# Three 256-column matmuls for a k tile in place of one of 512 and one of 256, with no folding of halves

## The chip, the cores and the metric

The kernel runs on one core of a Trainium2 chip. The metric is the device time of one execution in microseconds (us), the median over three timed runs. One more execution, on its own, is taken by the hardware profiler; its trace is what the views quoted here show.

## The reference, cut to what matters

One layer of an encoder block on 256 tokens of width 2048, in float32: a combined input projection, windowed attention with 12 query and 4 key/value heads of 128, a Fourier group, an output projection with a residual, and a feed-forward part with a width-3 convolution on its gate.

```python
h = _rmsnorm(x, norm1_g)
proj = h @ w_in                       # q 1536, k 512, v 512, u 512 columns
a = _rmsnorm(_window_attention(q, k, v, sink), attn_out_g)
f = _rmsnorm(_fourier_mix(u, w_fourier), fourier_out_g)
x = x + jnp.concatenate([a, f], axis=-1) @ w_out
up = _rmsnorm(x, norm2_g) @ w_up      # gate and value, 5504 columns each
gate = depthwise_conv(gate, dw_w, width 3) + dw_b
x = x + (gelu(gate) * val) @ w_down
return _rmsnorm(x, normf_g)
```

## The kernel before, in words

Every product is made of three, so that it comes out near float32: each operand is held as a high part and a low part (type fp32r, four bytes an element), and high times high, high times low and low times high are summed in PSUM. Weights arrive as tiles of 128 x 2048 float32, one megabyte each (`raw`, three buffers). `split_parts` makes the parts from such a tile: ScalarE (ACT) copies it into the high part (L170) and VectorE (DVE) subtracts that from the tile into the low part (L171). Both parts lie in one buffer (`parts_tile`, three buffers): the high part begins at one of `PLACES`' first numbers, the low part 2048 elements and the second number behind the buffer's start, in elements of four bytes.

There are two kinds of product. In the first, `moving_weights` and the products of the down-projection (`by_parts`, L1019 to L1021), the weights stream through TensorE in 512 columns and the activations are loaded as the stationary operand. In the second, `still_weights`, it is the weights that are loaded, 128 x 128 at a time, and the activations that stream: 256 tokens. The second kind makes q and k (16 units, one for a head, in the order `QK_ORDER`) and gate and value (43 units each, one for 128 of the 5504 columns), which is 102 units in all. The activations `hT` (for q and k) and `hU` (for gate and value) hold, for each of the 16 k tiles, the 256 high columns and behind them the 256 low columns.

A unit of `still_weights` before the change does two matmuls for a k tile. One loads the high part of the weights and streams all 512 columns (L326), so that high times high lies in the left half of the PSUM bank and high times low in the right half. The other loads the low part and streams the 256 high columns into the left half (L328). `lag=4`, for q, k and the first gate after the pair, lets five high matmuls go before the first low one; at the end of such a unit five low ones stand in a row. Since the sum then lies in two halves, ScalarE copies the right half to SBUF and VectorE adds the left half to it: `qk_out` (L579, L581) and `scaled_sum` (L810, L812). After that keys are multiplied by `r1b`, gate and value by `r2b` (L813).

The order of the work is written out by hand. `unit` issues the matmuls of unit i and then what stands beside it: the steps of attention heads that are at other stages, and the splitting of the weights of unit i + 2. In the feed-forward part a list of items does the same, in which gate and value units take turns with the products of the down-projection (`PATTERN`); `ff_step` runs the posts of earlier items, `scaled_sum` one item behind its matmuls, `gate_conv` two behind, and splits the weights of item n + 2. Each engine does its instructions in the order in which they were issued.

Three other places stream 256 columns with a load for each matmul: the scores (L602, six a head), the values (L674, six a head) and the Fourier rows (L491, 24 in a row); the very last product of the kernel does it too (L1156 to L1158, in two pieces of 256 columns).

Of the kernel before, what the change touches and what calls it, by code (L numbers as in the profile page):

```python
# [8 lines left out]
F32 = mybir.dt.float32  # L9
F32R = mybir.dt.float32r  # L10
AF = mybir.ActivationFunctionType
ALU = mybir.AluOpType

P = 128
D = 2048
S = 256
NK = D // P
# [46 lines left out]
def ff_items():  # L64


    def ups(tiles):
        return [(kind, j) for j in tiles for kind in ("gate", "val")]

    items = ups(range(8))  # L70
    for g in range(N_GROUPS):
        todo = {
            "u": ups(range(8 * g + 8, 8 * g + 16)),
            "s": [("product", g, c, p) for c in range(2) for p in PRODUCTS[c]],
        }
        items += [todo[c].pop(0) for c in PATTERN]
        assert not any(todo.values())
    items += [("down", 0, c) for c in range(4)] + ups(LAST)
    items += [("down", 1, c) for c in range(4)] + [("last", c) for c in range(4)]
    return items  # L80
# [3 lines left out]
def block_kernel(  # L84
# [18 lines left out]
    nc = tc.nc  # L103
# [10 lines left out]
    def bank(pool, name):  # L114
        return pool.tile([P, 512], F32, tag=pool.name, name=name)
# [5 lines left out]
    items, up_index = ff_items(), {}  # L121
# [11 lines left out]
    raws, halves = {}, {}  # L133


    PLACES = {"still": (0, 16), "first": (16, 16), "moving": (0, 0), "product": (28, 28)}

    def parts_tile(name, place):
        t = wp.tile([P, 2 * 2048 + 128], F32R, tag="parts", name=name, bufs=3)
        oh, ol = PLACES[place]  # L140
        return t[:, oh : oh + 2048], t[:, 2048 + ol : 4096 + ol]

    def load(i, pieces=1):
        if i < len(units) and i not in raws:
            src, n, _ = units[i]
            raws[i] = wp.tile([P, 2048], F32, tag="raw", name=f"raw{i}", bufs=RAW)
            m = n // pieces
            for p in range(pieces):
                s = slice(p * m, (p + 1) * m)
                nc.sync.dma_start(raws[i][:, s], src[:, s])  # L150
                yield
# [28 lines left out]
    ph = pa.enter_context(tc.tile_pool(name="pa", bufs=1))  # L180
# [21 lines left out]
    first = load(0, 4)  # L202
# [50 lines left out]
    ps = bank(dn, "ps_warm")  # L253
# [58 lines left out]
                ps, ah, wl, start=False, stop=last and q == q0 + len(kk) - 1  # L312
            )

    def still_weights(hi, lo, ps, kk, lag=0):


        todo = [("hi", k) for k in kk[: lag + 1]]
        for n, k in enumerate(kk):
            todo.append(("lo", k))  # L320
            todo += [("hi", q) for q in kk[lag + 1 + n : lag + 2 + n]]
        for part, k in todo:
            h = hT[k // 4][:, k % 4, :]
            s = slice(k * P, (k + 1) * P)
            if part == "hi":
                nc.tensor.matmul(ps, hi[:, s], h, start=k == 0, stop=False)  # L326
            else:
                nc.tensor.matmul(  # L328
                    ps[:, 0:S], lo[:, s], h[:, 0:S], start=False, stop=k == NK - 1
                )  # L330

    def hk(k):
# [15 lines left out]
    before, beside, behind = {}, {}, {}  # L348

    def at(when, i, f, *a):  # L350
        when.setdefault(i, []).append((f, a))
# [5 lines left out]
    def unit(i, work):  # L357
        run(before, i)
        work(*halves.pop(i))
        run(beside, i)  # L360
        step(i)
        run(behind, i)
# [6 lines left out]
    for k in range(NK):  # L369
        c, q = k // 4, k % 4  # L370
# [4 lines left out]
        hi, lo = halves[c]  # L375
# [49 lines left out]
    r1b = ph.tile([P, S], F32, tag="r1b", name="r1b")  # L425
# [137 lines left out]
    for c in range(4):  # L563

        def work(hi, lo):
            for b in range(2):
                moving_weights(
                    hi, lo, 512, range(4 * c, 4 * c + 4), hk, b, ps_v[b], c == 0, c == 3
                )

        unit(N_V + c, work)


    qk_sb, st = {}, {}
    sq_a = ph.tile([P, S], F32, tag="sq", name="sq_a")

    def qk_out(kind, h, ps):
        tmp = ph.tile([P, S], F32, tag="tmp", name=f"tmp_{kind}{h}", bufs=2)
        nc.scalar.activation(tmp, ps[:, S : 2 * S], AF.Copy)  # L579
        add = ph.tile([P, S], F32, tag="add", name=f"add_{kind}{h}", bufs=2)  # L580
        nc.vector.tensor_tensor(add, ps[:, 0:S], tmp, ALU.add)  # L581
        if kind == "k":
            nc.vector.tensor_tensor(add, add, r1b, ALU.mult)
        st["add", kind, h] = add

    def qk_parts(kind, h):

# [99 lines left out]
    for i in range(N_QK, N_OUT + 8):  # L687
        heads = {i - s: h for (kind, h), s in slot_of.items() if kind == "q"}
        new = [kh for kh, s in slot_of.items() if i - s == 1]
        if 5 in heads:  # L690
            at(before, i, values, heads[5])
        if 4 in heads:
            at(before, i, turn, heads[4])
        if 2 in heads:
            at(before, i, scores, heads[2])
        if 3 in heads:
            at(beside, i, weigh, heads[3])
        for kind, h in new:
            at(beside, i, lambda k=kind, h=h: qk_out(k, h, st.pop(("ps", k, h))))
        if 5 in heads:  # L700
            at(beside, i, values_out, heads[5])
        if 4 in heads:
            at(beside, i, turn_out, heads[4])
        for kind, h in new:
            at(beside, i, qk_parts, kind, h)
        if 2 in heads:
            at(beside, i, scores_out, heads[2])
            at(behind, i, exps, heads[2])

    fourier_channels_steps()  # L710
    for n, (kind, h) in enumerate(QK_ORDER):

        def work(hi, lo):
            ps = st["ps", kind, h] = bank(mm, f"ps_{kind}{h}")
            still_weights(hi, lo, ps, range(NK), lag=4)

        unit(N_QK + n, work)

# [49 lines left out]
    for n, (c, kq) in enumerate(OUT_ORDER):  # L768
        i = N_OUT + n
# [14 lines left out]
        if kq >= 2:  # L784
            part = "a" if kq == 2 else "f"
            ps = ps_a[c] if kq < 3 else ps_a[c, "f"]
# [15 lines left out]
    fp = ctx.enter_context(tc.tile_pool(name="fp", bufs=2))  # L802
    hT[:] = hT2
    r2b = fp.tile([P, S], F32, tag="r2b", name="r2b", bufs=1)
# [1 line left out]
    gate_out, sums_of, act = {}, {}, {}  # L806

    def scaled_sum(ps, name):
        tmp = fp.tile([P, S], F32, tag="ftmp", name=f"ft_{name}")
        nc.scalar.activation(tmp, ps[:, S : 2 * S], AF.Copy)  # L810
        add = fp.tile([P, S], F32, tag="fadd", name=f"fa_{name}", bufs=3)
        nc.vector.tensor_tensor(add, ps[:, 0:S], tmp, ALU.add)  # L812
        nc.vector.tensor_tensor(add, add, r2b, ALU.mult)  # L813
        sums_of[name] = add

    def gate_conv(j):
# [83 lines left out]
    def ring_load():  # L900
        if ring_next[0] < len(ring):
            key = ring[ring_next[0]]
            ring_next[0] += 1
            ring_tiles[key] = fp.tile([P, 2048], F32, tag="rawd", name="rawd%d%d%s" % key)
            nc.sync.dma_start(ring_tiles[key], weights_of(*key))
# [174 lines left out]
    for q in range(2):  # L1080
        kind, j = items[q]
        ps = bank(mm, f"ps_{kind}{j}")
# [6 lines left out]
    for ps, hi, lo in pair:  # L1089
        still_weights(hi, lo, ps, range(12, NK))  # L1090
# [7 lines left out]
    for n, it in enumerate(items):  # L1098
        if n < 2:
            continue  # L1100
        if it[0] == "last":
            break
        if n in (8, 9):
            ring_load()
        if n == 13:
            pending.append(lambda: first_sums(0, 0))
        if it[0] in ("gate", "val"):
            kind, j = it
            ps = bank(mm, f"ps_{kind}{j}")
            still_weights(*halves.pop(up_index[n]), ps, range(NK), lag=4 if n == 2 else 0)  # L1110
            ff_step(n)
            up_posts(n, kind, j, ps)
            continue
        if it[0] == "product":
            kind, g, c, p = it
            end = g == N_GROUPS - 1
            if (c, p) in held:
                by_parts(held[c, p], parts[p], *halves.pop(it), g == 0, end)
            else:
                ps = bank(mm, f"ps_{p}{g}{c}")  # L1120
                by_parts(ps, parts[p], *halves.pop(it), True, True)
                at(beside, n + 1, product_out, g, c, p, ps)
            if end and p == "N4":
                at(behind, n + 1, shared_out, c)
        else:
            kind, g, c = it
            hi, lo = halves.pop(up_index[n])
            ps = [bank(mm, f"ps_l{g}{c}{b}") for b in range(2)]
            for b in range(2):
                moving_weights(hi, lo, 512, LATE[g], act.get, b, ps[b], True, True)  # L1130
            at(beside, n + 1, down_out, c, ps)
            if (g, c) == (0, 0):
                gfb = fp.tile([P, D], F32, tag="sumw", name="gfb", bufs=1)
                nc.gpsimd.dma_start(gfb, normf_g.partition_broadcast(P))
        ff_step(n)
# [3 lines left out]
    i = up_index[n]  # L1139
# [145 lines left out]
```

## Time and profile before

| what | us |
|---|---|
| median of 3 runs | 952.24 |
| lowest and highest | 951.86, 952.95 |
| the profiled execution, its own time | 953.02 |
| its span, first to last instruction | 951.2 |
| TensorE busy in it | 940.7 |
| VectorE busy | 744.8 |
| ScalarE busy | 540.3 |

PE is TensorE's matmuls, PEld its weight loads, DVE VectorE, ACT ScalarE, POOL GpSimd. A row of groups gives line, engine, operation, output and inputs, shapes and count, then busy us and mean ns of one, then the idle time before and what ended it. A row of the timeline gives start, duration, engine, line and what was done; the time from one start to the next is what a matmul costs in a stream, since matmuls overlap and their recorded ends are modelled. The granted TensorE clock was 0.998 of full speed over the span.

### The profile page before, as it was taken

How to read it: one execution, taken by the hardware profiler on the slowest of the kernel's cores; microseconds unless marked ns; L12 is line 12 of the kernel's file. 1: busy time of each engine (PE TensorE's matmuls, PEld its weight loads, DVE VectorE, ACT ScalarE, POOL GpSimd, SP SyncE). 2: the span in 40 equal slices, each digit the busy share in tenths (PEclk: the TensorE clock that was granted, in tenths of full speed). 3: DMA queues.
4: the chain of work that ended last, by engine and by line, in shares of the span. 5: the costliest groups of instructions: out<-in, count | busy, mean ns of one | idle time of the engine just before them, and what ended most of it. 6: DMA issues, size and time to landing. Idle time of an engine off the chain costs nothing.

```text
span 951.2 us, 12801 instructions
## 1 busy us (share of the span) xinstructions
PE 940.7 (99%) x5089; PEld 813.0 (85%) x5089; DVE 744.8 (78%) x924; ACT 540.3 (57%) x654; POOL 44.7 (5%) x59
## 2 busy tenths in 40 slices
PE   8999999999999999999999999999999999999996
PEld 7788999888888888888888888888888888888885
DVE  5667878667676779887898877998889979888774
ACT  5846666544464456655555555565556755653444
POOL 0000000000000000000000000000000000000003
PEclk9999999999999999999999999999999999999999
DMA  8844444445556675978687787777987696765542
GB/s 313 346 180 178 147 164 140 171 177 177 183 177 216 265 240 202 260 254 282 214 271 232 239 291 257 251 238 223 295 253 245 213 294 201 243 241 205 197 133 89
DMA packets 33548, 211.59 MB, mean 222 GB/s; under 512 B 3792, under 2 KB 4304, under 8 KB 9424
## 3 DMA queue, kind: packets, MB, share of 16 engines
q1 hardware_dynamic: 29744, 184.54, 52.1%
q0 software_dynamic: 3600, 26.22, 14.2%
q8 instruction: 40, 0.66, 0.2%
q14 instruction: 20, 0.16, 0.1%
q10 hardware_dynamic: 144, 0.01, 0.0%
HBM read 208.65 MB, written 2.10 MB: 222 GB/s over the span
## 4 chain that ended last, share of the span: by engine, by line
PE 92%; DVE 3%; DMA 2%; issue 1%; ACT 1%; SPq 0%; POOL 0%; ACTq 0%; POOLq 0%
PE ps_val L326 16%; PE ps_gate L326 16%; PE ps_val L328 8%; PE ps_gate L328 8%; PE ps_q L326 5%; PE ps_P L1020 3%; PE ps_P L1021 3%; PE ps_P L1019 3%; PE ps_q L328 2%; PE ps_a L311 2%; PE ps_a L309 2%; PE ps_a L310 2%; PE ps_N L1021 2%; PE ps_N L1020 2%; PE ps_N L1019 2%; DMA raw<-in_w_in 2%
## 5 line engine op out<-in xcount | busy, mean ns | idle before, releaser
L171 DVE TENSOR_TENSOR parts<-raw,parts 128x2048 fp32r<-128x2048 f32 (+3 forms) x145 | 313.1, 2159 | 62.5 <-ACT parts L170 62.5
L170 ACT ACTIVATE parts<-raw 128x2048 fp32r<-128x2048 f32 (+3 forms) x144 | 262.0, 1820 | 72.4 <-PE ps_l L311 25.9
L326 PE MATMUL ps_val<-hU,parts 128*128 128x512 f32 x688 | 236.2, 389 | 0.0
L326 PE MATMUL ps_gate<-hU,parts 128*128 128x512 f32 x688 | 235.8, 389 | 0.0
L328 PE MATMUL ps_val<-hU,parts 128*128 128x256 f32 x688 | 189.9, 276 | 0.0
L328 PE MATMUL ps_gate<-hU,parts 128*128 128x256 f32 x688 | 189.3, 276 | 0.0
L326 PEld LDWEIGHTS ps_val<-hU,parts 128*128 128x128 f32 x688 | 129.2, 188 | 26.6
L326 PEld LDWEIGHTS ps_gate<-hU,parts 128*128 128x128 f32 x688 | 129.1, 188 | 26.7
L328 PEld LDWEIGHTS ps_val<-hU,parts 128*128 128x128 f32 x688 | 129.2, 188 | 1.2 <-DVE parts L171 0.2
L328 PEld LDWEIGHTS ps_gate<-hU,parts 128*128 128x128 f32 x688 | 128.9, 188 | 1.2
L810 ACT ACTIVATE ft_g<-ps_gate 128x256 f32<-128x256 f32 x43 | 16.5, 384 | 116.6 <-PE ps_gate L328 116.6
L810 ACT ACTIVATE ft_v<-ps_val 128x256 f32<-128x256 f32 x43 | 16.5, 384 | 88.3 <-PE ps_val L328 88.3
L326 PE MATMUL ps_q<-hT,parts 128*128 128x512 f32 x192 | 61.3, 393 | 0.0
L1019 PE MATMUL ps_P<-parts_P,op_P 128*128 128x512 f32 x128 | 49.8, 389 | 0.0
L1020 PE MATMUL ps_P<-parts_P,op_P 128*128 128x512 f32 x128 | 49.8, 389 | 0.0
L1021 PE MATMUL ps_P<-parts_P,op_P 128*128 128x512 f32 x128 | 49.8, 389 | 0.0
L328 PE MATMUL ps_q<-hT,parts 128*128 128x256 f32 x192 | 45.5, 278 | 0.0
L916 DVE TENSOR_TENSOR parts_N<-sumw,parts_N 128x2048 fp32r<-128x2048 f32 x16 | 36.6, 2290 | 10.1 <-ACT parts_N L915 10.1
L326 PEld LDWEIGHTS ps_q<-hT,parts 128*128 128x128 f32 x192 | 35.2, 188 | 6.8
L309 PE MATMUL ps_a<-parts,cat 128*128 128x512 f32 x96 | 37.9, 394 | 0.0
L1021 PE MATMUL ps_N<-parts_N,op_N 128*128 128x512 f32 x96 | 37.5, 390 | 0.1
L311 PE MATMUL ps_a<-parts,cat 128*128 128x512 f32 x96 | 37.5, 390 | 0.0
(323 smaller groups left out, 1564.7 us busy)
## 6 DMA issues: line engine op xcount, KB each, us to landing
raw<-in_w_up SPq DMA_DIRECT2D x86, 1024.0 KB, 5.0
raw<-in_w_in SPq DMA_DIRECT2D x21, 1024.0 KB, 4.9
raw<-in_w_out SPq DMA_DIRECT2D x16, 1024.0 KB, 4.8
sumw<-in_w_down POOLq DMA_DIRECT2D x16, 1024.0 KB, 8.4
raw<-in_w_down_late SPq DMA_DIRECT2D x8, 1024.0 KB, 4.8
raw<-in_w_down_last SPq DMA_DIRECT2D x4, 768.0 KB, 4.2
raw<-in_w_in SPq DMA_DIRECT2D x8, 256.0 KB, 6.5
xs<-in_x SPq DMA_DIRECT2D x4, 512.0 KB, 11.1
```

What stands on the lines that cost most here:

```text
L170: nc.scalar.activation(hi[:, s], raw[:, s], AF.Copy)
L171: nc.vector.tensor_tensor(lo[:, s], raw[:, s], f32(hi[:, s]), ALU.subtract)
L309: nc.tensor.matmul(ps, ah, wh, start=first and q == q0, stop=False)
L310: nc.tensor.matmul(ps, al, wh, start=False, stop=False)
L311: nc.tensor.matmul(ps, ah, wl, start=False, stop=last and q == q0 + len(kk) - 1)
L326: nc.tensor.matmul(ps, hi[:, s], h, start=k == 0, stop=False)
L328: nc.tensor.matmul(ps[:, 0:S], lo[:, s], h[:, 0:S], start=False, stop=k == NK - 1)
L810: nc.scalar.activation(tmp, ps[:, S : 2 * S], AF.Copy)
L916: nc.vector.tensor_tensor(lo, src, f32(hi), ALU.subtract)
L1019: nc.tensor.matmul(ps, o[:, 0, p, :], hi[:, s], start=first and p == 0, stop=False)
L1020: nc.tensor.matmul(ps, o[:, 1, p, :], hi[:, s], start=False, stop=False)
L1021: nc.tensor.matmul(ps, o[:, 0, p, :], lo[:, s], start=False, stop=last and p == 3)
```

## The change

For q, k, gate and value each k tile now takes three matmuls of 256 columns, all summed in the same 256 columns of PSUM: high weights by high activations, high weights by low activations, low weights by high activations. Each matmul loads its own weights. The copy of the right half and the addition go: `scaled_sum` multiplies PSUM by `r2b`, keys are multiplied by `r1b` straight from PSUM, and the parts of a query are made straight from PSUM. The low parts of these weights lie 128 bytes further than 2048 elements from the buffer's start, where they lay 64 bytes further. `lag` is gone.

```diff
-    PLACES = {"still": (0, 16), "first": (16, 16), "moving": (0, 0), "product": (28, 28)}
+    PLACES = {"still": (0, 32), "first": (16, 16), "moving": (0, 0), "product": (28, 28)}
...
-    def still_weights(hi, lo, ps, kk, lag=0):
-        todo = [("hi", k) for k in kk[: lag + 1]]
-        for n, k in enumerate(kk):
-            todo.append(("lo", k))
-            todo += [("hi", q) for q in kk[lag + 1 + n : lag + 2 + n]]
-        for part, k in todo:
+    def still_weights(hi, lo, ps, kk):
+        for k in kk:
             h = hT[k // 4][:, k % 4, :]
             s = slice(k * P, (k + 1) * P)
-            if part == "hi":
-                nc.tensor.matmul(ps, hi[:, s], h, start=k == 0, stop=False)
-            else:
+            for n, (w, o) in enumerate([(hi, 0), (hi, S), (lo, 0)]):
                 nc.tensor.matmul(
-                    ps[:, 0:S], lo[:, s], h[:, 0:S], start=False, stop=k == NK - 1
+                    ps[:, 0:S], w[:, s], h[:, o : o + S],
+                    start=k == 0 and n == 0, stop=k == NK - 1 and n == 2,
                 )
...
-    def qk_out(kind, h, ps):
-        tmp = ph.tile([P, S], F32, tag="tmp", name=f"tmp_{kind}{h}", bufs=2)
-        nc.scalar.activation(tmp, ps[:, S : 2 * S], AF.Copy)
-        add = ph.tile([P, S], F32, tag="add", name=f"add_{kind}{h}", bufs=2)
-        nc.vector.tensor_tensor(add, ps[:, 0:S], tmp, ALU.add)
+    def qk_out(kind, h):
+        ps = st.pop(("ps", kind, h))[:, 0:S]
         if kind == "k":
-            nc.vector.tensor_tensor(add, add, r1b, ALU.mult)
-        st["add", kind, h] = add
+            add = ph.tile([P, S], F32, tag="add", name=f"add_{kind}{h}", bufs=2)
+            nc.vector.tensor_tensor(add, ps, r1b, ALU.mult)
+            ps = add
+        st["add", kind, h] = ps
...
-            still_weights(hi, lo, ps, range(NK), lag=4)
+            still_weights(hi, lo, ps, range(NK))
...
     def scaled_sum(ps, name):
-        tmp = fp.tile([P, S], F32, tag="ftmp", name=f"ft_{name}")
-        nc.scalar.activation(tmp, ps[:, S : 2 * S], AF.Copy)
         add = fp.tile([P, S], F32, tag="fadd", name=f"fa_{name}", bufs=3)
-        nc.vector.tensor_tensor(add, ps[:, 0:S], tmp, ALU.add)
-        nc.vector.tensor_tensor(add, add, r2b, ALU.mult)
+        nc.vector.tensor_tensor(add, ps[:, 0:S], r2b, ALU.mult)
         sums_of[name] = add
...
-            still_weights(*halves.pop(up_index[n]), ps, range(NK), lag=4 if n == 2 else 0)
+            still_weights(*halves.pop(up_index[n]), ps, range(NK))
```

More of the change, by code (lines that the diff above doesn't have):

```diff
@@ L698, in block_kernel @@
         for kind, h in new:
-            at(beside, i, lambda k=kind, h=h: qk_out(k, h, st.pop(("ps", k, h))))
+            at(beside, i, qk_out, kind, h)
         if 5 in heads:
```

## The prediction

> **What bounds the kernel now.** I read the page first: busy times, the clock, and the shares of the chain that ended last.
>
> ```profile
> span 951.2 us, 12801 instructions
> PE 940.7 (99%) x5089; PEld 813.0 (85%) x5089; DVE 744.8 (78%) x924; ACT 540.3 (57%) x654; POOL 44.7 (5%) x59
> PEclk9999999999999999999999999999999999999999
> PE 92%; DVE 3%; DMA 2%; issue 1%; ACT 1%; SPq 0%; POOL 0%; ACTq 0%; POOLq 0%
> ```
>
> TensorE is busy for 99% of the span, its clock granted at nine tenths or more all along, and it carries 92% of the chain. But a busy share does not say that TensorE waits for nobody, so I looked next at who it waited for, in the waits of PE and PEld. Apart from the first tens of microseconds, where the first weights land, these three are the only ones that VectorE's work for the changed part can touch (columns: who waited for whom, total us, times, longest):
>
> ```profile
> PEld ps_N L1021 <- DVE parts_N L916: 0.5, 1, 0.5
> PEld ps_val L328 <- DVE parts L171: 0.2, 1, 0.2
> ...
> PE ps_l L309 <- DVE xs L1026: 0.2, 1, 0.2
> ```
>
> So VectorE's work reaches TensorE for 0.9 us in all. The kernel is bound by how fast TensorE can be fed with matmuls, and the question is what the changed stream costs from one matmul's start to the next. The timeline of PE at the start and the end of one gate unit and one product:
>
> ```profile
> 501.57 0.39 PE L326 MATMUL ps_gate<-hU,parts 128*128 128x512 f32 x1
> 501.80 0.28 PE L328 MATMUL ps_gate<-hU,parts 128*128 128x256 f32 x1
> 501.91 0.39 PE L326 MATMUL ps_gate<-hU,parts 128*128 128x512 f32 x1
> ...
> 507.01 0.39 PE L1019 MATMUL ps_N<-parts_N,op_N 128*128 128x512 f32 x1
> ...
> 509.73 0.39 PE L326 MATMUL ps_val<-hU,parts 128*128 128x512 f32 x1
> ```
>
> From 501.57 to 507.01 the unit takes 5.44 us, 0.340 for each of 16 k tiles. Twelve matmuls of 512 columns take 509.73 - 507.01 = 2.72, 0.2267 each. That leaves 0.340 - 0.2267 = 0.1133 for the one of 256: half of 0.2267, so in this alternation time goes by columns and the loads are hidden.
>
> **The change, part by part: the matmuls.** A k tile streams 512 + 256 = 768 columns before and 3 x 256 = 768 after. By columns alone nothing changes. What is added is one matmul and one weight load for a k tile. The load cannot be saved because the same high part comes twice: the scores also use the same weights twice in a row, then others, and load every time (the one line's instructions):
>
> ```profile
> L602 PEld LDWEIGHTS ps_s<-kT,qT x72: 187/189/192, 75.5 to 172.5; 128*128 128x128 f32 x72
> L602 PE MATMUL ps_s<-kT,qT x72: 278/282/368, 75.7 to 172.6; 128*128 128x256 f32 x72
> ```
>
> 72 loads for 72 matmuls. Now look at when loads happen, in the timeline of PEld for the gate unit above:
>
> ```profile
> 501.80 0.19 PEld L326 LDWEIGHTS ps_gate<-hU,parts 128*128 128x128 f32 x1
> 501.92 0.19 PEld L328 LDWEIGHTS ps_gate<-hU,parts 128*128 128x128 f32 x1
> 502.14 0.19 PEld L326 LDWEIGHTS ps_gate<-hU,parts 128*128 128x128 f32 x1
> ```
>
> A load starts when the matmul before its own starts. In the alternation the load of the low part has 0.227 of a 512-column matmul to hide in, that of the high part only 0.113. After the change every load has 0.113. So the rows to price it are those where 256-column matmuls with their own loads follow each other: the end of a query unit with `lag`, then values and scores; the Fourier rows in the chain; the last product:
>
> ```profile
> 136.56 0.76 PE L328 MATMUL ps_q<-hT,parts 128*128 128x256 f32 x5
> 137.15 0.40 PE L674 MATMUL ps_o<-pt,v_hi 128*128 128x256 f32 x2
> ...
> 137.87 0.88 PE L602 MATMUL ps_s<-kT,qT 128*128 128x256 f32 x6
> 138.59 1.31 PE L326 MATMUL ps_k<-hT,parts 128*128 128x512 f32 x5
> ...
> 49.01 2.88 PE ps_f L491 x24
> ...
> 941.27 0.28 PE L1157 MATMUL ps_e<-hi,act 128*128 128x256 f32 x1
> ...
> 942.47 0.28 PE L1158 MATMUL ps_e<-lo,act 128*128 128x256 f32 x1
> ```
>
> Six scores take 138.59 - 137.87 = 0.72, 0.120 each; six values 137.87 - 137.15 = 0.72, again 0.120; 24 Fourier rows 2.88, 0.120; ten of the last product 942.47 - 941.27 = 1.20, 0.120. Five low parts of the very weights in question take 137.15 - 136.56 = 0.59, which is 0.113 for the first (its successor's load still profits from the long matmul ahead) and 0.119 for each of the other four. Four places in different buffers agree on 0.0067 more than a column count gives. I take 0.113 for the first and 0.120 for each of the other 47 matmuls of a unit: 5.75 us in place of 5.44.
>
> The units are 102 and the k tiles 1632, from these groups (mean ns is the second number after the bar):
>
> ```profile
> L326 PE MATMUL ps_val<-hU,parts 128*128 128x512 f32 x688 | 236.2, 389 | 0.0
> L326 PE MATMUL ps_gate<-hU,parts 128*128 128x512 f32 x688 | 235.8, 389 | 0.0
> L328 PE MATMUL ps_gate<-hU,parts 128*128 128x256 f32 x688 | 189.3, 276 | 0.0
> L326 PE MATMUL ps_q<-hT,parts 128*128 128x512 f32 x192 | 61.3, 393 | 0.0
> L328 PE MATMUL ps_q<-hT,parts 128*128 128x256 f32 x192 | 45.5, 278 | 0.0
> L326 PE MATMUL ps_k<-hT,parts 128*128 128x512 f32 x64 | 20.4, 393 | 0.0
> ```
>
> 688 + 688 + 192 + 64 = 1632, and 1632 / 16 = 102. Units of q and k run a little slower than 5.44: their matmuls are 393 - 389 = 4 ns longer for 256 wide ones and 278 - 276 = 2 ns for 256 narrow ones, 1.5 us in sum; that is the row of five and five that `lag` makes, and it goes. Before: 102 x 5.44 + 1.5 = 556.4. After: 102 x 5.75 = 586.5. Difference **+30.1 us**, all of it on the path, since TensorE is the path. Bounds: 0.118 for every matmul (the mean of the five low ones) gives 48 x 0.118 x 102 = 577.7, +21; 0.1205 gives 590.0, +34.
>
> **The copies and additions.** They go from 86 gate and value units and 16 of q and k:
>
> ```profile
> L812 DVE TENSOR_TENSOR fa_g<-ps_gate,ft_g 128x256 f32<-128x256 f32 x43 | 18.1, 422 | 24.1 <-ACT ft_g L810 24.1
> L810 ACT ACTIVATE ft_g<-ps_gate 128x256 f32<-128x256 f32 x43 | 16.5, 384 | 116.6 <-PE ps_gate L328 116.6
> ```
>
> 102 x 0.42 = 43 us less on VectorE, 102 x 0.38 = 39 us less on ScalarE. Nearly all of it lies beside TensorE's work, so it is worth at most the 0.9 us of waits above; I count -0.5, because a slower TensorE lets VectorE catch up. If TensorE should stay as fast, VectorE's waits go as well. Multiplying by `r2b` straight from PSUM costs what the addition cost, which also read PSUM. The additions' buffer and the PSUM banks come free earlier; nobody waited for either.
>
> **`lag` gone.** The low part of the first k tile is wanted 0.23 us into a unit, not at the sixth matmul. Gate and value units had no lag but for one, and for the unit at 501.57 VectorE had the low part finished at 498.17 + 2.29 = 500.46:
>
> ```profile
> 498.17 2.29 DVE L171 TENSOR_TENSOR parts<-raw,parts 128x2048 fp32r<-128x2048 f32 x1
> ```
>
> That is 1.3 us before 501.80, in the stretch where VectorE is fullest. I count it at nothing; its cover is the two units between splitting and use, and without it each unit could lose up to the 0.9 us that `lag` covered, 16 us over 17 units. The 64 further bytes of the low parts cost no instruction; what they may do is a rival's matter.
>
> Sum: 30.1 - 0.5 is about +30. The profiled execution took 953.0 (1.8 more than its span), which gives 983; the median of 952.2 gives **982**. A measurement of this kernel can tell about 0.2%, 1.9 us, from no change.
>
> **Rivals.** *The loads fit* (other sign). Where the two parts of the weights lie against the streaming activations is not the same in any of my four rows as after the change, and the low part's place is moved in this very edit. If the 0.0067 is a clash between load and stream that this place avoids, then each matmul costs 0.1133, a unit 5.44, the stream 554.9: -1.5, and the waits another -0.9 at most: 952.2 - 2.4 = 949.8, near 950. It decides at 0.1138: up to there, 48 x 102 x 0.0005 = 2.4 us are covered by what is saved. For it: in the alternation a load that has just 0.113 is in time, 16 times a unit, with the high part at its unchanged place. Against it: there each is followed by one that has 0.227, and with the second tight load in a row the spacing goes to 0.119. I give it 0.38, 0.27 of that faster by over 0.2% and 0.11 within 0.2%, as the saving is close to the line.
>
> The Trainium skill has a rule that speaks for this rival: "TensorE: Matmul & The Clock Gate", section "LDWEIGHTS (loading the stationary operand)", gives a load as its columns divided by 1.2 in ns. For 128 columns that is an estimate of 107 ns, which would fit under a matmul of 113, and by it the result would be 950. The rows above with 0.120 do not agree with it as long as loads follow each other this closely.
>
> *Something between*: the clash is eased but not gone, 0.115 to 0.118 a matmul, +8 to +21: 960 to 973. Chance 0.07.
>
> *Loads in a row do not overlap*: each took 0.19 in the rows above. If a matmul cannot start before its load's recorded end and loads follow one another, a k tile costs 3 x 0.188 = 0.564, and 1632 x 0.224 = 366 us are added: 1318. The scores speak against it, 0.120 with loads of 0.189. Chance 0.01.
>
> *VectorE had been the hidden bound*, so that 43 us less of it shows: 952.2 - 5 or more. The waits of 0.9 us in all speak against it; it lies within the 0.27.
>
> **How the numbers follow.** Forecast 0.54, with its own range 973 to 986 (from +21 to +34); fitting loads 0.38; between 0.07; loads in a row 0.01. Slower by over 0.2%: 0.54 + 0.07 + 0.01 = 0.62. Leaving out the fitting loads would leave out 0.38, so the range goes from them to the forecast's upper end: 948.5 (1.5 under 950, for savings in q and k that I undercounted) to 986.
>
> **What would show it.** In the profile after, PE and PEld rows x5089 become x6721 (+1632). A gate unit on the timeline takes 5.75 from its first start to the next item's. The spacing inside it is 0.120, and PE stays at 99%; VectorE's busy time falls by some 43 us and ScalarE's by 39, their shares further. Wrong: a spacing of 0.113 and a unit of 5.44 mean that the loads fit; a PEld wait for VectorE's `parts` at L171 of several microseconds means that `lag` had been needed.

## The result and the profile after

The changed kernel takes 959.73 us, the kernel before 952.29 (medians of four runs each): a ratio of 1.0077, 95% interval 1.006 to 1.0095. That is +7.4 us, slower as forecast, but a quarter of the +30 that was forecast, and outside the 973 to 986 given for the forecast's own case. The profiled execution took 959.13 with a span of 957.4.

The page of the changed kernel, the same lines as before the change:

```profile
span 957.4 us, 15831 instructions
PE 947.8 (99%) x6721; PEld 884.8 (92%) x6721; DVE 703.0 (73%) x822; ACT 510.5 (53%) x552; POOL 44.6 (5%) x59
PE 96%; DMA 2%; ACT 0%; DVE 0%; issue 0%; POOL 0%; ACTq 0%; POOLq 0%; SPq 0%
```

TensorE does 1632 matmuls and loads more, VectorE is busy for 41.8 us less and ScalarE for 29.8 less, and TensorE still carries the chain. By the starts of their matmuls the 102 units together take 556.8 us before and 564.1 after, 7.3 more. What VectorE made TensorE wait for at L916, L171 and L1026 in the body of the kernel is gone; what is left of PEld's waits for VectorE and ScalarE lies in the first 30 us, where the first weights land. Its longest rows:

```profile
PEld ps_u L311 <- DVE parts L171: 1.7, 4, 0.5
PEld ps_u L309 <- ACT parts L170: 1.2, 2, 0.7
```

So where do the 6 us of span come from? I cut the span at the same five instructions in both traces: the first gate unit after the pair, the first unit behind the first product, the first late down-projection, the first unit of the last stretch, the first matmul of the last product. The timeline of PE, of the kernel before and then of the changed one:

```profile
272.96 0.48 PE L326 MATMUL ps_gate<-hU,parts 128*128 128x512 f32 x1
...
368.29 0.39 PE L326 MATMUL ps_val<-hU,parts 128*128 128x512 f32 x1
...
850.18 0.39 PE L309 MATMUL ps_l<-parts,act 128*128 128x512 f32 x1
...
872.43 0.39 PE L326 MATMUL ps_gate<-hU,parts 128*128 128x512 f32 x1
...
926.88 0.39 PE L1156 MATMUL ps_e<-parts,act 128*128 128x512 f32 x1
```

```profile
273.32 0.36 PE L322 MATMUL ps_gate<-hU,parts 128*128 128x256 f32 x1
...
373.19 0.28 PE L322 MATMUL ps_val<-hU,parts 128*128 128x256 f32 x1
...
854.64 0.39 PE L309 MATMUL ps_l<-parts,act 128*128 128x512 f32 x1
...
876.63 0.28 PE L322 MATMUL ps_gate<-hU,parts 128*128 128x256 f32 x1
...
932.64 0.39 PE L1147 MATMUL ps_e<-parts,act 128*128 128x512 f32 x1
```

| stretch | before, us | after, us | difference |
|---|---|---|---|
| up to gate 1 | 272.96 | 273.32 | +0.36 |
| 17 gate and value units, then the first product | 95.33 | 99.87 | +4.54 |
| 61 units in turn with products | 481.89 | 481.45 | -0.44 |
| late down-projection | 22.25 | 21.99 | -0.26 |
| 6 units, late down-projection | 54.45 | 56.01 | +1.56 |
| last product and the end | 24.32 | 24.76 | +0.44 |

The longest stretch, with most of the units, costs nothing. Two short ones carry most of the loss. (The first row hides some: the q and k units take 1.1 us longer there and the pair 0.2, but in this execution the work ahead of them ended 0.8 sooner.) The timeline shows what differs; a row that stands for a whole unit has x48, and the next row's start less its own is what the unit took. First three units of the slow stretch, then its last unit and the first product behind it, which ends where the row at 373.19 above begins, then units of the long stretch:

```profile
284.81 5.87 PE L322 MATMUL ps_gate<-hU,parts 128*128 128x256 f32 x48
290.52 5.87 PE L322 MATMUL ps_val<-hU,parts 128*128 128x256 f32 x48
296.23 5.87 PE L322 MATMUL ps_gate<-hU,parts 128*128 128x256 f32 x48
...
364.71 5.87 PE L322 MATMUL ps_gate<-hU,parts 128*128 128x256 f32 x48
370.41 0.40 PE L1010 MATMUL ps_P<-parts_P,op_P 128*128 128x512 f32 x1
...
479.28 5.60 PE L322 MATMUL ps_gate<-hU,parts 128*128 128x256 f32 x48
484.72 5.60 PE L322 MATMUL ps_val<-hU,parts 128*128 128x256 f32 x48
490.16 1.07 PE L322 MATMUL ps_gate<-hU,parts 128*128 128x256 f32 x8
```

5.71 us here, 0.119 a matmul; 5.44 there, 0.1133 a matmul, in units of the same code. By their starts 66 of the 102 units take 5.44 to 5.47, thirty take 5.70 to 5.79 (seven of q and k, and the 17 and the 6 of the two slow stretches), and six lie between. So the stream has two steady rhythms, and the questions are what allows the quick one and what chooses between them.

The starts of loads and matmuls, taken from the trace to the nanosecond, say where the difference lies. In both rhythms a load starts 2 to 5 ns behind the start of the matmul before it. In the quick one its own matmul starts 110 ns after the load on average, in the slow one 116 (112 to 122). The recorded duration of a load is the same in both, 0.19 us.

### The profile page after: what moved, and what is told of

It reads as the page before. It is cut to its first block, busy times and chain, and to the rows that moved or that the text cites. A ratio compares the mean times of both kernels' runs of the same rounds, so it can differ in the third digit from the quotient of the medians.

```text
span 957.4 us, 15831 instructions
## 1 busy us (share of the span) xinstructions
PE 947.8 (99%) x6721; PEld 884.8 (92%) x6721; DVE 703.0 (73%) x822; ACT 510.5 (53%) x552; POOL 44.6 (5%) x59
## 4 chain that ended last, share of the span: by engine, by line
PE 96%; DMA 2%; ACT 0%; DVE 0%; issue 0%; POOL 0%; ACTq 0%; POOLq 0%; SPq 0%
PE ps_gate L322 25%; PE ps_val L322 25%; PE ps_q L322 7%; PE ps_P L1010 3%; PE ps_P L1011 3%; PE ps_P L1012 3%; PE ps_k L322 2%; PE ps_a L311 2%; PE ps_a L309 2%; PE ps_a L310 2%; PE ps_N L1010 2%; PE ps_N L1012 2%; PE ps_N L1011 2%; DMA raw<-in_w_in 2%; PE ps_l L309 2%; PE ps_l L310 2%
## 5 line engine op out<-in xcount | busy, mean ns | idle before, releaser
L171 DVE TENSOR_TENSOR parts<-raw,parts 128x2048 fp32r<-128x2048 f32 (+3 forms) x145 | 313.1, 2159 | 76.7 <-ACT parts L170 76.3
L322 PE MATMUL ps_gate<-hU,parts 128*128 128x256 f32 x2064 | 244.5, 277 | 0.0
L322 PEld LDWEIGHTS ps_val<-hU,parts 128*128 128x128 f32 x2064 | 242.1, 188 | 2.2
L322 PE MATMUL ps_val<-hU,parts 128*128 128x256 f32 x2064 | 244.1, 277 | 0.0
L322 PE MATMUL ps_q<-hT,parts 128*128 128x256 f32 x576 | 69.5, 279 | 0.0
L322 PEld LDWEIGHTS ps_q<-hT,parts 128*128 128x128 f32 x576 | 67.9, 188 | 0.0
L906 ACT ACTIVATE parts_N<-sumw 128x2048 fp32r<-128x2048 f32 x16 | 30.7, 1917 | 35.7 <-PE ps_val L322 22.5
L309 PE MATMUL ps_a<-parts,cat 128*128 128x512 f32 x96 | 37.9, 395 | 0.0
L311 PE MATMUL ps_a<-parts,cat 128*128 128x512 f32 x96 | 37.5, 390 | 0.0
L310 PE MATMUL ps_a<-parts,cat 128*128 128x512 f32 x96 | 37.3, 389 | 0.0
L1010 PE MATMUL ps_N<-parts_N,op_N 128*128 128x512 f32 x96 | 37.3, 389 | 0.0
L1011 PE MATMUL ps_N<-parts_N,op_N 128*128 128x512 f32 x96 | 37.3, 389 | 0.0
L1012 PE MATMUL ps_N<-parts_N,op_N 128*128 128x512 f32 x96 | 37.3, 389 | 0.0
L804 DVE TENSOR_TENSOR fa_g<-ps_gate,r2b 128x256 f32<-128x256 f32 x43 | 18.1, 422 | 23.1 <-PE ps_gate L322 23.1
L1012 PEld LDWEIGHTS ps_P<-parts_P,op_P 128*128 128x128 f32 x128 | 24.0, 188 | 5.0
```

Of the source, the lines that this page charges most:

```text
L171: nc.vector.tensor_tensor(lo[:, s], raw[:, s], f32(hi[:, s]), ALU.subtract)
L309: nc.tensor.matmul(ps, ah, wh, start=first and q == q0, stop=False)
L310: nc.tensor.matmul(ps, al, wh, start=False, stop=False)
L311: nc.tensor.matmul(ps, ah, wl, start=False, stop=last and q == q0 + len(kk) - 1)
L322: nc.tensor.matmul(ps[:, 0:S], w[:, s], h[:, o : o + S], start=k == 0 and n == 0, stop=k == NK - 1 and n == 2,)
L804: nc.vector.tensor_tensor(add, ps[:, 0:S], r2b, ALU.mult)
```

## The experiments

Two theories. **Theory 1, the place:** whether a load fits under a matmul of 256 columns depends on where the weights' parts lie, against the streaming activations or against each other. **Theory 2, the inheritance:** at this place both rhythms hold themselves up, and a unit takes over that of the work before it. The rival to the second was that the slow stretches are slow for a reason of their own, such as transfers or the other engines. The three do not exclude each other, so each experiment changes one thing.

**The changed kernel with the low parts back at 64 bytes on.**

```diff
-"still": (0, 32)
+"still": (0, 16)
```

> The changed kernel with the low parts back at 64 bytes on (the only edit). Where the low part lies decides whether a load fits under a 256-column matmul (theory 1): no steady 0.1133 any more, 0.119 to 0.120 a matmul in nearly all 102 units, 5.70 to 5.76 a unit, about 980 us. The place plays no part, only what ran on TensorE before (theory 2): the same two rhythms in the same stretches as in the changed kernel, 959.7 us within 2.

Measured 975.71 us, ratio 1.0242 (1.0212 to 1.0271) to the kernel before. Its timeline in the stretch that had been quick:

```profile
488.93 5.82 PE L322 MATMUL ps_val<-hU,parts 128*128 128x256 f32 x48
494.58 5.82 PE L322 MATMUL ps_gate<-hU,parts 128*128 128x256 f32 x48
...
584.50 0.39 PE L1010 MATMUL ps_N<-parts_N,op_N 128*128 128x512 f32 x1
...
587.28 5.82 PE L322 MATMUL ps_val<-hU,parts 128*128 128x256 f32 x48
```

5.65 a unit, and 5.65 to 5.75 in every unit but the pair, whose pieces add up to the same: no unit is quick at this place. The place alone is worth 16 us, 13 of it in the units. Most of the rest is in the products behind them: the twelve matmuls of one take 587.28 - 584.50 = 2.78 here. In the changed kernel all products but the first take 2.72, and their own operands lie where they lie here. So the work in front of a matmul counts, and not its own operands alone. Theory 1 holds in that the place decides; its figures, 5.70 to 5.76 a unit and 980 us, were a little high.

**The kernel before with its low parts at 128 bytes on.**

```diff
-"still": (0, 16)
+"still": (0, 32)
```

> The kernel before with its low parts at 128 bytes on (the only edit). Theory 1 and theory 2 alike: each load that has only 0.113 us is followed by one that has 0.227, so the unit stays at 5.44 and the time at 952.3 within 1. If the new place by itself costs something, the unit is longer than 5.44 here too.

Measured 972.23 us, ratio 1.0205 (1.0175 to 1.0235): what both theories expected is missed by 20 us, and with it goes my belief that 512 and 256 columns in turn hide their loads anywhere. The case named last is what happened: the place by itself costs something. The timeline:

```profile
284.77 0.28 PE L328 MATMUL ps_gate<-hU,parts 128*128 128x256 f32 x1
284.88 0.40 PE L326 MATMUL ps_gate<-hU,parts 128*128 128x512 f32 x1
285.12 0.28 PE L328 MATMUL ps_gate<-hU,parts 128*128 128x256 f32 x1
```

A k tile takes 285.12 - 284.77 = 0.35, not 0.34; the 512 columns that took 0.227 take 0.24, though their successor's load has all of that to hide in. So the place does more than decide whether a load fits under 256 columns. Here too there is more than one rhythm: gate and value units take 5.64 or 5.65 up to the late down-projection, the last six 5.54 to 5.55, and so do nine of the sixteen q and k units. With the run above and the two kernels this makes a table of four: 512 + 256 at 64 bytes 952, at 128 bytes 972; three of 256 at 64 bytes 976, at 128 bytes 960. Neither half of the edit is good alone; each stream has its place.

**The three matmuls with the fold kept.**

```diff
-for n, (w, o) in enumerate([(hi, 0), (hi, S), (lo, 0)]):
-    nc.tensor.matmul(ps[:, 0:S], w[:, s], h[:, o : o + S], ...)
+for n, (w, o, to) in enumerate([(hi, 0, 0), (hi, S, S), (lo, 0, 0)]):
+    nc.tensor.matmul(ps[:, to : to + S], w[:, s], h[:, o : o + S], ...)
```

> The changed kernel's three matmuls of 256 columns at the same place, but high weights by low activations summed in the right half of the bank, and the copy and the addition kept. The stream of TensorE is the cause (both theories): 959.7 plus at most the 0.9 us of waits, 959 to 961.5. If the copies and additions had been worth more than their waits showed, or summing three in one place costs something, the time is 2 us or more off 959.7.

Measured 960.22 us, ratio 1.0079 (1.005 to 1.0108), as the changed kernel. From its page, its groups and its waits:

```profile
PE 948.0 (99%) x6721; PEld 884.9 (92%) x6721; DVE 744.9 (78%) x924; ACT 540.1 (56%) x654; POOL 44.6 (5%) x59
...
L322 PE MATMUL ps_gate<-hU,parts 128*128 128x256 f32 x2064 | 244.5, 277 | 0.0
...
PEld ps_N L1016 <- DVE parts_N L911: 0.5, 1, 0.5
```

VectorE and ScalarE work as long as before the change, and the matmuls are those of the changed kernel. The copies and additions lie beside TensorE's work, as the prediction said. The wait for `parts_N` that the change had removed is back, the last row, and it is half a microsecond.

**Two units in the old manner, as seeds.** Gate 1 and gate 40 stand at the heads of the two slow stretches.

```diff
+SEEDS = ("g1", "g40")
...
-still_weights(*halves.pop(up_index[n]), ps, range(NK))
+work = still_halves if seed else still_weights   # still_halves: 512 and 256
+work(*halves.pop(up_index[n]), ps, range(NK))
```

> The changed kernel, but two of its 86 gate and value units (gate 1, the first after the pair, and gate 40, the first of the last stretch) in the old manner, 512 and 256 columns with the fold; all units after them are unchanged. Theory 2 (a rhythm is taken over from what ran before and kept): the 22 units behind the two, at 5.71 in the changed kernel, take 5.44; about 23 x 0.267 = 6 us less, 953.6. If these stretches are slow for a reason of their own (transfers, the other engines, where the buffers lie): only the two units gain, 0.5 us, 959.2.

Measured 959.74 us, ratio 1.0074 (1.0045 to 1.0103). No gain: 5.71 behind the seed still.

```profile
279.67 5.87 PE L339 MATMUL ps_val<-hU,parts 128*128 128x256 f32 x48
285.38 5.87 PE L339 MATMUL ps_gate<-hU,parts 128*128 128x256 f32 x48
```

The kernel before with its low parts at 128 bytes shows why this proves little: the seeds' parts too lay at 128 bytes, where 512 + 256 is not quick itself (the seeds took 5.64 and 5.54). They had no quick rhythm to hand on. So the same again, with the parts of the two seeds, and of nothing else, at 64 bytes:

```diff
+"seed": (0, 16)
...
-units.append((w_up[...], 2048, "still"))
+units.append((w_up[...], 2048, "seed" if this unit is in SEEDS else "still"))
```

> As the run with two units in the old manner, but the parts of those two units lie as in the kernel before (low parts 64 bytes on), where 512 and 256 columns run at 5.44 a unit; in that run the two took 5.64 and 5.54, so what followed them had not taken over a quick rhythm. Theory 2 (a rhythm is taken over and kept): the units behind the two now take 5.44, about 23 x 0.267 = 6 us less than the changed kernel, 953.6. If the stretch itself is slow, or the three-matmul stream falls into the slow rhythm by itself after the old one: 5.71 again behind them, 959.2.

Measured 953.93 us, ratio 1.0018 (1.0006 to 1.0029). The units behind gate 1 and behind gate 40:

```profile
279.11 5.62 PE L340 MATMUL ps_val<-hU,parts 128*128 128x256 f32 x48
284.56 5.60 PE L340 MATMUL ps_gate<-hU,parts 128*128 128x256 f32 x48
290.00 5.60 PE L340 MATMUL ps_val<-hU,parts 128*128 128x256 f32 x48
...
877.75 5.60 PE L340 MATMUL ps_val<-hU,parts 128*128 128x256 f32 x48
883.19 5.60 PE L340 MATMUL ps_gate<-hU,parts 128*128 128x256 f32 x48
```

5.44 to 5.45 in all 21 of them. These two runs differ by 64 bytes in the low parts of two units, and the 21 units that come after, whose instructions, buffers and neighbours on the other engines are the same, go from 5.71 to 5.44. Theory 2 holds from one unit to the next, and the stretch itself is cleared. In its units this kernel is still 1.3 us behind the kernel before, most of it in q and k, seven of whose units are still slow.

**Three other places for the changed kernel.**

```diff
-"still": (0, 32)
+"still": (16, 48)     # and (28, 60), and (0, 0)
```

> The changed kernel with both parts of q, k, gate and value 64 bytes further (high 64, low 64 and 128): the distance between the parts is kept, that to the streaming activations is not. If only the distance between the parts decides: the two rhythms of the changed kernel, 959.7 within 2. If the distance to the activations decides: another figure, between 950 (all at 5.44) and 985 (all at 5.76).

> As the run before, both parts 112 bytes further, the offset at which the products' parts lie. Same alternatives: 959.7 within 2 if only the distance between the parts decides, else between 950 and 985.

> The changed kernel with the low parts at 0 bytes on, 2048 elements behind the high ones. With 64 bytes on a unit took 5.65 everywhere and with 128 bytes 5.44 or 5.71. If a period of 128 bytes in the distance decided, this would be as the changed kernel, 959.7 within 2; otherwise another figure, and the place at 128 bytes is one among several.

Measured 982.63 (ratio 1.0324, 1.0294 to 1.0354), 984.40 (1.0342, 1.0312 to 1.0372) and 976.64 us (1.0261, 1.0231 to 1.0291). One stretch of each, in this order:

```profile
288.50 5.89 PE L322 MATMUL ps_gate<-hU,parts 128*128 128x256 f32 x48
294.23 5.88 PE L322 MATMUL ps_val<-hU,parts 128*128 128x256 f32 x48
299.94 5.88 PE L322 MATMUL ps_gate<-hU,parts 128*128 128x256 f32 x48
```

```profile
288.63 5.92 PE L322 MATMUL ps_gate<-hU,parts 128*128 128x256 f32 x48
294.39 5.92 PE L322 MATMUL ps_val<-hU,parts 128*128 128x256 f32 x48
```

```profile
287.95 5.82 PE L322 MATMUL ps_gate<-hU,parts 128*128 128x256 f32 x48
293.61 5.82 PE L322 MATMUL ps_val<-hU,parts 128*128 128x256 f32 x48
```

Nearly all gate and value units take 5.71 to 5.73 in the first; in the second 5.76, but 5.73 behind a product; and 5.65 in the third (5.653, where the rounded starts above give 5.66). The first two runs keep the distance between the parts and move both, by 64 and by 112 bytes, against the activations: so that distance counts. The third moves the low part alone by 128 bytes: a period of 128 bytes is ruled out. Of the five places tried only that of the change has units of 5.44; the quickest whole units elsewhere are three of q at 0 bytes, at 5.53.

**All places moved, all distances kept.**

```diff
-vec = base.tile([P, V_N], F32, tag="vec", name="vec")
+vec = base.tile([P, V_N + 8], F32, tag="vec", name="vec")
```

> The changed kernel with 32 bytes of padding behind the vectors' buffer, so that the activations, all weights' parts and nearly all else lie 32 bytes further: every distance between operands is kept, none of the places is. If distances between the operands alone decide: the two rhythms in the same units as in the changed kernel, 959.7 within 2. If the places themselves count, each operand's against a line of the memory: other spacings, also for the 512-column matmuls of the products, which took 0.227 in every kernel so far.

Measured 960.05 us, ratio 1.0078 (1.0060 to 1.0097), with 5.71 and 5.44 in the same units as in the changed kernel:

```profile
280.53 5.87 PE L322 MATMUL ps_val<-hU,parts 128*128 128x256 f32 x48
286.24 5.87 PE L322 MATMUL ps_gate<-hU,parts 128*128 128x256 f32 x48
...
480.70 5.60 PE L322 MATMUL ps_gate<-hU,parts 128*128 128x256 f32 x48
486.14 5.60 PE L322 MATMUL ps_val<-hU,parts 128*128 128x256 f32 x48
```

The vectors' buffer itself begins where it began, and all the kernel's buffers behind it lie 32 bytes further. As far as one such shift can tell, it is the distances between the operands that decide and not their places.

**The version that this points to.** q, k, the first pair, gate 1 and gate 40 as in the kernel before, with their places; the other 82 units as in the changed kernel.

> The version that the runs so far point to: q and k, the first pair, gate 1 and gate 40 as in the kernel before (512 and 256 columns, low parts 64 bytes on, fold kept), the other 82 gate and value units as in the changed kernel. Theory 2 (a rhythm is taken over and kept): all units behind gate 1 at 5.44, q and k at the 5.47 to 5.69 that they took before; against the kernel before only the waits of about 1 us go, 951 us. If falling into the slow rhythm is a matter of chance at each entry: a stretch of 16 or of 5 units at 5.71, 952.4 to 956.

Measured 952.35 us over eleven runs, the kernel before 952.55 over fifteen: ratio 1.000, 0.9991 to 1.0009. Its first two units behind gate 1 and its page:

```profile
278.96 5.60 PE L340 MATMUL ps_val<-hU,parts 128*128 128x256 f32 x48
284.40 5.60 PE L340 MATMUL ps_gate<-hU,parts 128*128 128x256 f32 x48
...
PE 940.8 (99%) x6401; PEld 864.1 (91%) x6401; DVE 710.8 (75%) x842; ACT 517.6 (54%) x572; POOL 44.5 (5%) x59
```

Every unit takes what the forecast by theory 2 said: 5.44 to 5.46 behind gate 1, and in q and k what they took before. VectorE has 34 us less to do than in the kernel before, and the time is the same. The expected 951 is missed: the microsecond of waits that should have gone does not show in the median. No version here beats the kernel before; three matmuls at their best are as good as 512 + 256 at theirs.

## Why the prediction was right and wrong

**Right:** that TensorE is the path and columns alone change nothing; that the load comes again for the same weights (x6721 on PEld), and that loads in a row overlap, or 5.44 for 48 of them could not be; that copies and additions are worth almost nothing, for which the run with the fold kept stands; that nothing waits for the low part without `lag`: no such wait at q, k, gate or value is left. (The 16 us named as its risk are 15 by the prediction's own 0.9 us times 17 units.) VectorE's 43 us less came out at 41.8. ScalarE's 39 came out at 29.8: the recorded durations of its instructions do fall by 39, but they overlap each other, and busy time counts an overlap once.

**The step that failed** is the pricing of the matmuls: "I take 0.113 for the first and 0.120 for each of the other 47 matmuls of a unit". Measured, it is 0.119 in 30 units and 0.1133 in 66. The sum's term of +30.1 came out at +7.3. The rows that gave 0.120 agreed with each other, and I read that as a property of loads in a row, with 0.118 as the least it could be. For this stream it goes by the place of the weights and by the work in front: at four of five places it takes 0.118 to 0.120 in nearly all units, and two of these kernels take 982.6 and 984.4, next to the forecast of 982. At the place that the change chose, 0.1133 is possible. The sign was right because 30 units did run near the spacing forecast; in the last version, where no unit of three matmuls does so, the time is that of the kernel before.

**The rival** that the loads fit looked at the right thing (the place of the weights' parts) and had the right spacing, and 0.38 was not a foolish chance for it. Its price of 950 took for granted that the quick rhythm holds everywhere once it is possible. That the work in front chooses the rhythm was in neither case. The case between, "0.115 to 0.118 a matmul", has the mean nearly right (66 units at 0.1133 and 30 at 0.119), and that is luck: it spoke of a clash that is half eased, and two whole rhythms stand side by side.

**A second wrong belief** stood in the same part: "in this alternation time goes by columns and the loads are hidden". It is true at 64 bytes on; at 128 the same alternation costs 20 us more. The prediction treated the 64 bytes as something that could only help or do nothing; changed by themselves they hurt.

The Trainium skill's rule in "TensorE: Matmul & The Clock Gate", section "LDWEIGHTS (loading the stationary operand)", is columns divided by 1.2, which gives an estimate of 107 ns for a load. The quick rhythm agrees, with a load every 113 ns. The slow rhythm does not follow from it: the same loads then come every 119 ns.

**What stays open:** which distances are good and why. The traces show when loads and matmuls start, not what they meet in memory, so a clash between load and stream is not shown. By the kernel's strides the distance between weights and activations changes by 1536 bytes from one k tile to the next and by 16,896 from one buffer of parts to the next, both multiples of 512, and in the long stretch the spacing stays at 0.113 or 0.114; what changed it were steps of 64 to 128 bytes. Also what chooses the rhythm where a stretch begins. The first product behind the slow units is slow itself, 373.19 - 370.41 = 2.78, and the unit behind it is quick all the same; the late down-projection ends with 512 columns at 0.227, and the unit behind it is slow. That q and k units fall into either rhythm, by what the heads' work before them leaves, was seen but not tried by itself.

## What to carry to other kernels

Where TensorE is the path and every matmul loads its own weights, treat the place of the operands against each other as a parameter of its own: a place tuned for one order of matmuls can cost 2% under another, so tune it again with the order, and never price an edit from rows whose operands lie elsewhere without giving the other price a range. Look at the spacing unit by unit before taking a mean: two steady values in identical code can mean, as here, a state that is handed on, and then the unit in front is where to act. And work taken off engines that nobody waits for (34 to 42 us of VectorE here) bought nothing.

## What the runs showed of the hardware that I had not expected

- The spacing of identical matmuls with their own loads depends on the byte distances between the loaded and the streamed operand: 5.44, 5.65, 5.71 or 5.76 us for 48 of them, with no wait in the trace at these units. Even 512 columns take 0.24 instead of 0.227 at a bad distance.
- At one distance two rhythms, 0.1133 and 0.119 a matmul, each last for 16 units, over 90 us, until another kind of work comes between; 64 bytes in where one earlier unit's low part lay chose which. Products of 512 columns, whose own operands lie alike in the kernels with three matmuls at 128 and at 64 bytes, took 2.72 us behind quick units and 2.77 or 2.78 behind slower ones.
- Moving nearly everything by 32 bytes left every unit as it was.
